# Unread products on TensorE in its waits ahead of the output stage, the expert layers and the second projection

## The chip, the cores and the metric

The kernel runs on one core of one Trainium2 chip. The number that counts is the device time of one execution in microseconds (us). The kernel before takes 3481.51 us (median of 3 runs, 3471.72 to 3489.32).

Engines are named as in the profile: PE is TensorE's stream of matrix products, PEld its loads of the stationary operand, DVE is VectorE, ACT ScalarE, POOL GpSimd, SP the engine that issues most DMAs. Each engine works its instructions in order, and they wait for one another through semaphores.

## The reference, cut to what matters

Two layers over 1024 latent tokens and 256 context tokens, width 1024, all in float32. Each layer is a mixer followed by a mixture of experts:

```python
# layer 0: mixer -> output projection;  layer 1: w_in -> windowed attention -> w_out
x_lat = x_lat + mod_l[2] * o_lat
x_lat = x_lat + mod_l[5] * _ec_moe(_modulate(_rms_norm(x_lat, norm_ffn[i]), mod_l[3], mod_l[4]),
                                   moe_router[i], moe_w1[i], moe_w3[i], moe_w2[i])

def _ec_moe(h, router, w1, w3, w2):     # every expert picks its own best tokens
    aff = softmax(h @ router)           # (tokens, 16 experts)
    gate, idx = top_k(aff.T, 2 * tokens / 16)
    xe = h[idx]
    return scatter_add(idx, (silu(xe @ w1) * (xe @ w3)) @ w2 * gate)
```

So an expert layer can't gather its tokens until the affinities of all tokens are known and sorted: 128 latent tokens for each expert in both layers, and 32 context tokens in layer 0.

## The kernel before, in words

The 1280 tokens are ten tiles of 128 (two of context, eight latent). The stages follow each other in time: a head and the first input projection; the two recurrent mixers and their scan (to 1223 us); the **output stage** of layer 0, which normalizes the mixers' outputs, multiplies by the output weights and computes the router's affinities (to about 1460); the **experts of layer 0** (to 2232); the **second projection**, of layer 1 (to about 2455); attention with its output products (to about 2850); the **experts of layer 1**, and the final norm.

Weights and activations are split into a high and a low half (`split_hl`, L1222 on ACT and L1223 on DVE), and a product is the sum of three products of halves. Those halves have the type float32r. Transposes against the identity matrix `K.ident`, the normalizing products (`post_rwkv`, L1238 and L1243) and the router's products (L1434) use plain float32.

What sets the order around the change: in these stages PE's instructions stand in the order in which the code issues them (`manual_schedule`); the other engines' order is made by a scheduler. The four places are these.

- **Ahead of the output stage.** `block(1)` starts the loads of the scan's results (`s_y`, `s_gb`, `s_o`) for two tiles, and POOL adds the two directions (L1235). Then four generators `post_rwkv` (L1238: a product for the mean; L1243: one for the variance) and two `post_gdn` (L1277: transposes) run, and the output weights `wo` are split. Only then do the output products (L1383) begin.
- **Ahead of the experts of layer 0.** After the last output product the loop over `late` runs what is left of the last two tiles: `ps_af` (L1446, transposes the affinities of a tile), then for the last tile `ps_hT` (L1426, 2 x 4 transposes), `ps_rt` (L1434, 8 router products) and its `ps_af`. DVE sorts in between (`topk_list`, L1459 to L1464). `topk_out` then transposes indices and gates (`ps_tk`, L1521), POOL gathers the tokens by them (L1561, `xe`; L1566, `xce` for context), PE transposes them (`ps_x`, L1580) and the first products of expert 0 begin (`ps_h`, L1611).
- **Ahead of the second projection.** After the last products of the experts (`ps_yc`, L1668) their results are added to `s_x` in memory; then a tile is read back, normalized, transposed (`ps_h`, L1807) and multiplied (`ps_qkv`, L1830; 24 products for a context tile), while the weights `wih`/`wil` are split.
- **Ahead of the experts of layer 1.** The same as in layer 0, without context tokens: `ps_af`, the sort on DVE, `ps_tk`, the gather, `ps_x`, `ps_h`.

Of the kernel before, what the change touches and what calls it, by code (L numbers as in the profile page):

```python
# [9 lines left out]
F32 = mybir.dt.float32  # L10
# [35 lines left out]
def dap(t, off, dims):  # L46
    return bass.AP(tensor=t.tensor, offset=t.offset + off, ap=[list(d) for d in dims])
# [8 lines left out]
def log_exp_table(K):  # L56

    K.table = K.tc.keep_in_program_order(K.nc.scalar.preload_act_table_set("natural_log_exp_and_others")).ins
# [168 lines left out]
def norm_cols(K, pool, layer, norm, ms, mh, tag):  # L227

    nc = K.nc
    G = pool.tile([128, 2, 8, 2], F32, name="G" + tag, bufs=1)  # L230
    for hf in range(2):
        k = slice(4 * hf, 4 * hf + 4)
        nc.vector.scalar_tensor_tensor(
            G[:, 0, k], K.modT[layer][:, ms // 2, :, (ms % 2) * 2 + hf, :], 1.0,
            K.P(norm, 8 * layer + 4 * hf, 4)[:, :, None].to_broadcast([128, 4, 2]), op0=OP.add, op1=OP.mult)
        nc.vector.tensor_copy(G[:, 1, k], K.modT[layer][:, mh // 2, :, (mh % 2) * 2 + hf, :])
    return G
# [982 lines left out]
def split_hl(K, hi, lo, src):  # L1220

    K.nc.scalar.activation(hi, src, AF.Copy)  # L1222
    K.nc.vector.tensor_sub(lo, src, hi)  # L1223
# [59 lines left out]
def turns(posts):  # L1283

    r, g = posts[:4], posts[4:]
    return [r[0], r[1], r[0], r[2], r[1], r[3], r[2], g[0], r[3], g[1]]
# [42 lines left out]
        behind(K, K.nc.sync.dma_start(t[:, k], rows_ap(W, 128 * k * D, 128, D)), last.ins.name)  # L1329


def split_raw(K, wp, raw, name):
    hi = wp.tile([128, 8, D], F32R, name=name + "h")
    lo = wp.tile([128, 8, D], F32R, name=name + "l")
    for k in range(8):
        split_hl(K, hi[:, k], lo[:, k], raw[:, k])
    return hi, lo
# [771 lines left out]
def body(tc, A, out, stop=None, mk=None):  # L2109
    nc = tc.nc  # L2110
    K = Ctx()
    K.nc, K.tc, K.pinned = nc, tc, set()
    with tc.tile_pool(name="consts", reuse_waits="tile", bufs=1) as cp, \
# [85 lines left out]
        with tc.tile_pool(name="moe_io", reuse_waits="tile", bufs=1) as mp:  # L2199
            K.mp = mp  # L2200
            m5 = [None, None]
            with tc.tile_pool(name="post", reuse_waits="tile", bufs=1) as p, \
                    tc.tile_pool(name="ps2", reuse_waits="tile", bufs=2, space=PSUM) as ps2, \
                    tc.tile_pool(name="ps1", reuse_waits="tile", bufs=2, space=PSUM) as ps1:
                log_exp_table(K)
                rt = p.tile([128, 8, 16], F32, name="router")
                nc.sync.dma_start(rt, dap(A["moe_router"], 0, [[16, 128], [2048, 8], [1, 16]]))
                g2 = {}
                nrm = norm_cols(K, mp, 0, "nffn", 4, 3, "f0")
                aff = tp.tile([16, T], F32, name="aff")  # L2210
                tkc = tp.tile([16, 2, 32], F32, name="tkc")
                fill = Fill()
                top = LatTop(K, tp, aff[:, NCTX:], fill, 7)
                late = {}

                def block(b):
                    mh = p.tile([128, 8, 256], F32R, name="mh", tag="mh", bufs=2)
                    ml = p.tile([128, 8, 256], F32R, name="ml", tag="ml", bufs=2)
                    posts = [post_rwkv(K, p, ps1, mh, ml, ct, 256 * b, 256, 0) for ct in range(4)] \
                        + [post_gdn(K, p, ps1, mh, ml, 2 * b + i, 128 * i) for i in range(2)]  # L2220
                    for g in posts:
                        next(g)
                    return mh, ml, turns(posts)

                def rest(o, tt):
                    for _ in range(4):
                        next(o)
                        yield
                    if tt == 1:
                        fill.add(topk_list(K, tp, aff[:, :NCTX], 0, 32, tkc, "c"))  # L2230
                    if tt > 1:
                        top.tile_done(tt)

                with tc.manual_schedule(engines={mybir.EngineType.PE}):
                    nxt = block(1)
                    for g in nxt[2]:
                        next(g)
                    wh, wl = split_raw(K, p, wo, "wo")
                    rawp.close()
                    op = wop.enter_context(tc.tile_pool(name="rows", reuse_waits="tile", bufs=1, side="right"))  # L2240
                    for s in (0, 1):
                        g2[s], = bcast_mods(K, A, 0, s, p, p, ps1, (2,), None, f"o{s}")

                    for at in range(NT):
                        tt = (at + 2) % NT
                        b, i = divmod(tt, 2)
                        if i == 0:
                            mh, ml, _ = nxt
                            q = []
                            if b > 0:  # L2250
                                nxt = block((b + 1) % (NT // 2))
                                q = nxt[2]
                        src = rows_ap(A["ctx"], tt * 128 * D, 128, D) if tt < 2 else \
                            rows_ap(A["x"], (tt - 2) * 128 * D, 128, D)
                        o = slice(128 * i, 128 * i + 128)
                        og = out_tile(K, p, op, ps2, ps1, lambda k, mh=mh, ml=ml, o=o: (mh[:, k, o], ml[:, k, o]), wh, wl, tt, src, g2[int(tt < 2)], nrm, rt, aff, 3, 4)
                        r = rest(og, tt)
                        for k in range(8):
                            next(og)
                            for x in late.pop(8 * at + k, ()):  # L2260
                                next(x, None)
                            if q and k in PSLOT:
                                next(q.pop(0))
                            fill.step(FRATE)
                        for x in RSLOT if at < RCUT else RLAST:
                            late.setdefault(8 * (at + 1) + x, []).append(r)
                        if at == 1:
                            for s in (1, 0):
                                m5[s], = bcast_mods(K, A, 0, s, mp, p, ps1, (5,), None, f"t{s}")
                    for k in sorted(late):  # L2270
                        for x in late[k]:
                            next(x, None)
                lat_sel = top.result(ps1)
                ctx_sel = topk_out(K, tp, ps1, tkc, 32, 4, "c")
            if stop == "out0":
                return
            wop.close()
            with tc.tile_pool(name="moe", reuse_waits="tile", bufs=1) as p, tc.tile_pool(name="mps", reuse_waits="tile", bufs=1, space=PSUM) as ps:
                Moe(K, A, 0, p, ps, lat_sel, ctx_sel, m5, nrm).run()
        if stop == "moe0":  # L2280
            return
        with ExitStack() as kvs:
# [4 lines left out]
            with tc.tile_pool(name="proj", reuse_waits="tile", bufs=1) as p, tc.tile_pool(name="ps2", bufs=3, space=PSUM) as ps2, \  # L2287
                    tc.tile_pool(name="ps1", reuse_waits="tile", bufs=3, space=PSUM) as ps1, \
                    tc.tile_pool(name="psC", reuse_waits="tile", bufs=1, space=PSUM) as psC:
                AT.p = p  # L2290
                afill = Fill()
                pre = stack.enter_context(ExitStack())
                pp = pre.enter_context(tc.tile_pool(name="pre", reuse_waits="tile", bufs=1, side="right"))
                for jj in (1, 2):
                    afill.add(ada_part(K, A, 1, jj, pp, psC))

                def mid():
                    afill.drain()
                    pre.close()
                    AT.kp = kvs.enter_context(tc.tile_pool(name="keys", reuse_waits="tile", bufs=1, side="right"))  # L2300
                    AT.keys(0)
                log_exp_table(K)
                wh, wl = load_split(K, p, A["o_w_in"], D, 1536, "wi", [(k, 0, 128, 128 * k) for k in range(8)], 3, stage=pp)
                mods = norm_cols(K, p, 1, "nmix", 1, 0, "i1")
                with tc.manual_schedule(engines={mybir.EngineType.PE}):
                    AT.project([0, 1] + list(range(2, NT)), wh, wl, mods, ps2, ps1, afill, mid)
                AT.keys(1)
            if stop == "proj":
                return
            with tc.tile_pool(name="tail1", reuse_waits="tile", bufs=1, side="right") as tp, \  # L2310
# [15 lines left out]
                top = LatTop(K, tp, aff, fill, 7, True)  # L2326
# [6 lines left out]
                    top.tile_done(n + 2)  # L2333
                with tc.manual_schedule(engines={mybir.EngineType.PE}):
                    AT.run(ps2, ps1, pso, out_n, fill, split)
                lat_sel = top.result(ps1)
            kvs.close()
            if stop == "out1":
                return
# [34 lines left out]
```

## Time and profile before

| | |
|---|---|
| median of the runs | 3481.51 us |
| lowest and highest | 3471.72 and 3489.32 us |
| the profiled execution: its time | 3488.81 us |
| the profiled execution: its span | 3487.0 us |
| mean granted TensorE clock | 0.945 of full |
| PE busy | 3127.7 us, 90% of the span |
| DVE busy | 2438.2 us, 70% |
| ACT busy | 2074.6 us, 59% |

A row of the timeline is: start in us, duration in us, engine, source line, operation, the tile written <- the tiles read, shape, and how many such records were merged (x8). In brackets stands the idle time of the engine ahead of it and what ended it. A row of the windows is: the stretch, its length, the busy time of each engine in it with the number of its records, the granted TensorE clock as a share of full speed, the share of the DMA engines that was busy, and GB/s. [...] A busy PE isn't a PE at its peak, since a product's duration holds its latency; how long a product occupies PE is read from the starts and ends of its neighbours.

### The profile page before, as it was taken

The page shows a single profiled execution, that of the slowest core. Times are in us where ns is not written, and L with a number is a line of the kernel's source. Part 1 is how long each engine was busy: PE and PEld are TensorE (multiplying, and loading weights), DVE is VectorE, ACT ScalarE, POOL GpSimd, SP SyncE. Part 2 cuts the span into 40 slices and gives each one's busy share as a digit, 9 for nine tenths or more (in the row PEclk, how much of TensorE's full clock was granted, in tenths as well). Part 3 has the DMA queues.
Part 4 walks back from the last instruction along what each step waited for, and adds up shares of the span by engine and source line. Part 5 has one row for each costly group of instructions (what it writes and reads, how often), then busy time and mean ns, then how long its engine had stood idle before and what let it go on. Part 6 is the DMA issues. An engine that isn't in the chain of part 4 may idle for free. (4 is left out here: it accounts for less than half of the span.)

```text
span 3487.0 us, 60267 instructions
## 1 busy us (share of the span) xinstructions
PE 3127.7 (90%) x23392; PEld 2393.5 (69%) x23392; DVE 2438.2 (70%) x4066; ACT 2074.6 (59%) x3548; POOL 726.7 (21%) x716
## 2 busy tenths in 40 slices
PE   5999899995879878699999999799699958999997
PEld 3866667775768757567666767467577746888885
DVE  4268884666534457877777777634876787999998
ACT  4255454332434455477777667534688838888886
POOL 1133332222333343201111110011233310010101
PEclk9999999897889989799999999899899979999998
DMA  5256656666999765578888887662311058999995
GB/s 194 75 181 197 191 194 201 204 187 123 202 221 199 169 218 169 187 254 298 299 286 282 307 287 283 221 212 95 83 49 49 34 205 303 395 384 392 386 380 208
DMA packets 480161, 767.80 MB, mean 220 GB/s; under 512 B 231836, under 2 KB 318532, under 8 KB 472708
## 3 DMA queue, kind: packets, MB, share of 16 engines
q1 hardware_dynamic: 434640, 601.05, 51.5%
q0 software_dynamic: 41648, 151.55, 13.9%
q10 hardware_dynamic: 3587, 11.36, 1.1%
q8 instruction: 184, 3.01, 0.4%
q14 instruction: 102, 0.83, 0.1%
HBM read 631.48 MB, written 132.38 MB: 219 GB/s over the span
## 5 line engine op out<-in xcount | busy, mean ns | idle before, releaser
L1223 DVE TENSOR_TENSOR ulo<-raw,uhi 128x1024 fp32r<-128x1024 f32 x768 | 898.0, 1219 | 84.1 <-ACT uhi L1222 69.7
L1222 ACT ACTIVATE uhi<-raw 128x1024 fp32r<-128x1024 f32 x768 | 790.6, 1073 | 196.6 <-PE ps_y L1662 89.2
L1611 PE MATMUL ps_h<-uhi,xh 128*128 128x512 f32 x1024 | 329.0, 399 | 2.1 <-ACT uhi L1222 2.0
L1611 PE MATMUL ps_h<-ulo,xh 128*128 128x512 f32 x1024 | 319.3, 392 | 3.7 <-DVE ulo L1223 3.0
L1611 PE MATMUL ps_h<-uhi,xl 128*128 128x512 f32 x1024 | 318.6, 392 | 0.0
L1678 POOL DMA_INDIRECT s_x<-yo,idxl x31 | 49.2, 1588 | 945.0 <-DVE yo L1674 945.0
L1611 PEld LDWEIGHTS ps_h<-ulo,xh 128*128 128x128 f32 x1024 | 190.4, 188 | 53.9 <-DVE ulo L1223 12.7
L1611 PEld LDWEIGHTS ps_h<-uhi,xh 128*128 128x128 f32 x1024 | 186.2, 188 | 51.0 <-ACT uhi L1222 8.7
L1611 PEld LDWEIGHTS ps_h<-uhi,xl 128*128 128x128 f32 x1024 | 191.2, 188 | 40.6
L354 PE MATMUL ps_in<-hl,whi 128*128 128x512 f32 x512 | 173.0, 411 | 0.0
L354 PE MATMUL ps_in<-hh,whi 128*128 128x512 f32 x512 | 172.4, 413 | 0.0
L354 PE MATMUL ps_in<-hh,wlo 128*128 128x512 f32 x512 | 171.9, 410 | 0.0
L1662 PE MATMUL ps_y<-uhi,th 128*128 128x512 f32 x512 | 162.1, 397 | 0.7 <-ACT tc L1648 0.6
L1662 PE MATMUL ps_y<-ulo,th 128*128 128x512 f32 x512 | 159.9, 393 | 0.1
L1662 PE MATMUL ps_y<-uhi,tl 128*128 128x512 f32 x512 | 158.1, 390 | 0.0
L1584 ACT ACTIVATE xv<-ps_x,Gf 128x128 f32<-128x128 f32 x256 | 96.9, 471 | 67.0 <-PE ps_x L1580 67.0
L1962 POOL TENSOR_SCALAR pe<-pe,ast 128x640 f32<-128x640 f32 (+1 forms) x48 | 90.2, 1879 | 185.9 <-DVE ast L1961 88.0
L1976 PE MATMUL ps_pT<-ident,pe 128*128 128x128 f32 x608 | 95.9, 282 | 35.1 <-ACT pT L1980 17.2
L852 DVE TENSOR_TENSOR invt<-invB,invX 128x112 f32<-128x112 f32 (+27 forms) x248 | 102.0, 411 | 29.9 <-DMA invB<-s_L 24.6
L1662 PEld LDWEIGHTS ps_y<-uhi,th 128*128 128x128 f32 x512 | 93.7, 188 | 38.9 <-ACT uhi L1222 12.0
L1949 DVE CUSTOM_DVE_ANT_0 pe<-ps_s,amask,sink 128x640 f32<-128x640 f32 (+2 forms) x128 | 103.4, 809 | 24.2 <-PE ps_s L1942 22.8
L1617 PE MATMUL ps_hc<-raw,xc 128*32 128x512 f32 x1024 | 119.6, 596 | 0.0
(505 smaller groups left out, 7276.7 us busy)
## 6 DMA issues: line engine op xcount, KB each, us to landing
raw<-in_moe_w_dram SPq DMA_DIRECT2D x384, 1024.0 KB
ada_w<-in_ada_w_dram SPq DMA_DIRECT2D x48, 1024.0 KB
wraw<-in_e_w_in_dram SPq DMA_DIRECT2D x32, 512.0 KB
s_rk<-arbk POOLq DMA_DIRECT2D x16, 1024.0 KB, 5.2
kq<-s_kq SPq DMA_DIRECT2D x20, 512.0 KB
s_x<-ox POOLq DMA_DIRECT2D x18, 512.0 KB, 3.0
s_h<-ot POOLq DMA_DIRECT2D x18, 512.0 KB, 3.9
s_rkv<-rkv POOLq DMA_DIRECT2D x12, 640.0 KB, 3.9
```

What stands on the lines that cost most here:

```text
L354: nc.tensor.matmul(ps, l[:, k, :], r[:, k, a:a + m], start=(k == 0 and n == 0), stop=(k == 7 and n == 2))
L852: nc.vector.tensor_mul(t, B[:N, k, k + 1:, None].to_broadcast([N, r, c]), X[:N, k, None, 0:c].to_broadcast([N, r, c]))
L1222: K.nc.scalar.activation(hi, src, AF.Copy)
L1223: K.nc.vector.tensor_sub(lo, src, hi)
L1584: nc.scalar.activation(v[:, q], pt[:, q], AF.Identity, bias=self.nrm[:, 1, k, 0:1], scale=self.nrm[:, 0, k, 0:1])
L1611: nc.tensor.matmul(pl[m][n], l[:, k], r[:, 512 * n:512 * n + 512], start=(k == 0 and i == 0), stop=(k == 7 and i == 2))
L1617: nc.tensor.matmul(pc[32 * g:32 * g + 32], xc[:, k_], rs[g // 2][:, 512 * (g % 2):512 * (g % 2) + 512], start=(k_ == 0), stop=(k_ == 7), s ...
L1662: nc.tensor.matmul(py[n], l[:, k], r[:, 512 * n:512 * n + 512], start=(k == 0 and i == 0), stop=(k == 7 and i == 2))
L1678: nc.gpsimd.indirect_dma_start(out=K.s_x[1], out_offset=bass.IndirectOffsetOnAxis(ap=idx[:, e:e + 1], axis=0), in_=yo, in_offset=None, com ...
L1949: nc.vector.tensor_tensor_reduce(pe[:, a:b], sc[:, 512 - nl + a:512 - nl + b], self.mask[:, m:m + b - a], 1.0, low, OP.add, OP.min, st[:, ...
L1962: (nc.vector if n < NV else nc.gpsimd).tensor_scalar(pes[0][:, :nk], pes[0][:, :nk], st[:, 4, 0:1], None, op0=OP.mult)
L1976: nc.tensor.transpose(pt[:, k, i_], pes[i_][:, 128 * (c + k):128 * (c + k) + 128], K.ident)
```

## The change

A new helper issues `n` products of the 128 x 128 identity matrix with itself, in plain float32, into one PSUM tile that nothing reads. It is called at the four places: 36 products ahead of the first normalizing products of the output stage; 16 ahead of every late step and 24 more at the end of that loop; 120 ahead of the second projection; 225 between the last `ps_af` of attention and `ps_tk`, and 40 between `ps_tk` and `ps_x`. In all 557.

```diff
+def warm(K, ps, n, tag="aux"):
+
+    t = ps.tile([128, 128], F32, name="ps_warm", tag=tag)
+    for _ in range(n):
+        K.nc.tensor.matmul(t, K.ident, K.ident, start=True, stop=True)
...
                 with tc.manual_schedule(engines={mybir.EngineType.PE}):
                     nxt = block(1)
+                    warm(K, ps1, 36, "post")
                     for g in nxt[2]:
                         next(g)
...
                     for k in sorted(late):
                         for x in late[k]:
+                            warm(K, ps1, 16, "post")
                             next(x, None)
+                    warm(K, ps1, 24, "post")
                 lat_sel = top.result(ps1)
...
                 with tc.manual_schedule(engines={mybir.EngineType.PE}):
+                    warm(K, ps1, 120)
                     AT.project([0, 1] + list(range(2, NT)), wh, wl, mods, ps2, ps1, afill, mid)
...
                     AT.run(ps2, ps1, pso, out_n, fill, split)
-                lat_sel = top.result(ps1)
+                    warm(K, ps1, 225)
+                    lat_sel = top.result(ps1)
+                    warm(K, ps1, 40)
```

On PE the instructions stand as follows ahead of the experts of layer 0, from the last output products to the first transposed tokens; before:

```order
L1383 MATMUL ps_out<-woh,ml 128x512 x2
L1446 MATMUL ps_af<-ident,sm 16x128
L1426 MATMUL ps_hT<-ident,ot 128x128 x8
L1434 MATMUL ps_rt<-router,ohT 128x16 x8
L1446 MATMUL ps_af<-ident,sm 16x128
L1521 MATMUL ps_tk<-ident,tk_12561 128x16 x2
L1521 MATMUL ps_tk<-ident,tkr 128x16 x2
L1580 MATMUL ps_x<-ident,xe 128x128 x8
```

and with the change, on the same engine at the same place (line numbers are 7 higher behind the new helper; `ps_warm` is its tile):

```order
L1390 MATMUL ps_out<-woh,ml 128x512 x2
L1336 MATMUL ps_warm<-ident 128x128 x16
L1453 MATMUL ps_af<-ident,sm 16x128
L1336 MATMUL ps_warm<-ident 128x128 x32
L1433 MATMUL ps_hT<-ident,ot 128x128 x4
L1336 MATMUL ps_warm<-ident 128x128 x16
L1433 MATMUL ps_hT<-ident,ot 128x128 x4
L1336 MATMUL ps_warm<-ident 128x128 x16
L1441 MATMUL ps_rt<-router,ohT 128x16 x8
L1336 MATMUL ps_warm<-ident 128x128 x16
L1453 MATMUL ps_af<-ident,sm 16x128
L1336 MATMUL ps_warm<-ident 128x128 x40
```

Six runs of the new products, 136 in all, now stand ahead of `ps_tk`, between instructions that depend on one another through DVE and ACT. Ahead of the experts of layer 1, on PE, before:

```order
L1446 MATMUL ps_af<-ident,sm 16x128
L1521 MATMUL ps_tk<-ident,tk_22859 128x16 x2
L1580 MATMUL ps_x<-ident,xe 128x128 x16
L1611 MATMUL ps_h_26931<-uhi,xh 128x512
L1611 MATMUL ps_h_26932<-uhi,xh 128x512
```

and with the change, on the same engine at the same place:

```order
L1453 MATMUL ps_af<-ident,sm 16x128
L1336 MATMUL ps_warm<-ident 128x128 x225
L1528 MATMUL ps_tk<-ident,tk_23161 128x16 x2
L1336 MATMUL ps_warm<-ident 128x128 x40
L1587 MATMUL ps_x<-ident,xe 128x128 x16
```

Nothing but the new products moved on PE here. POOL's order is unchanged; on DVE, ACT and SP a few instructions near the four places change places with a neighbour (in the second projection ACT takes four of the eight `wih` ahead of the first tile's work).

## Rows read from the trace of the kernel before

**Rows 1.** The head of the page.

```profile
span 3487.0 us, 60267 instructions
```

**Rows 2.** Windows, one ahead of each of the four places.

```profile
1230.00:1250.00 20.00, 10.67 (x25) 5.69 (x25) 14.86 (x26) 11.68 (x39) 9.77 (x9) 0.50 0.76 247
1440.00:1470.00 30.00, 12.63 (x53) 9.64 (x53) 20.40 (x74) 11.30 (x31) 6.17 (x7) 0.50 0.75 274
2245.00:2258.00 13.00, 6.94 (x19) 5.09 (x20) 7.32 (x6) 11.90 (x20) 0.00 (x0) 0.50 0.95 361
2840.00:2886.00 46.00, 8.79 (x38) 7.51 (x39) 30.87 (x99) 4.73 (x14) 2.73 (x4) 0.50 0.67 258
```

**Rows 3.** Timeline of PE, in the output stage and at the end of attention.

```profile
1258.98 0.63 PE L1383 MATMUL ps_out<-woh,ml 128*128 128x512 f32 x2
1259.45 0.59 PE L1238 MATMUL ps_mean<-py,hmean 128*128 128x256 f32 x2
1259.69 0.81 PE L1383 MATMUL ps_out<-woh,mh 128*128 128x512 f32 x2
...
2823.95 1.03 PE L1426 MATMUL ps_hT<-ident,ot 128*128 128x128 f32 x8
...
2826.20 1.91 PE L1434 MATMUL ps_rt<-router,ohT 128*128 128x16 f32 x16
```

**Rows 4.** Timeline of PE, ahead of the output stage.

```profile
1222.15 1.04 PE L1168 MATMUL ps_o<-Y,at 64*64 64x128 f32 x16
1230.73 1.22 PE L1238 MATMUL ps_mean<-py,hmean 128*128 128x256 f32 x2 [7.54 <-POOL py L1235]
```

**Rows 5.** Timeline of PE, ahead of the experts of layer 0.

```profile
1434.23 0.28 PE L1446 MATMUL ps_af<-ident,sm 128*16 128x128 f32 x1 [0.81 <-DVE sm L1443]
1440.90 1.97 PE L1426 MATMUL ps_hT<-ident,ot 128*128 128x128 f32 x8 [6.40 <-DVE ot L1418]
1443.62 3.59 PE L1434 MATMUL ps_rt<-router,ohT 128*128 128x16 f32 x16 [0.74 <-ACT ohT L1429]
...
1455.48 0.36 PE L1521 MATMUL ps_tk<-ident,tk 16*128 16x16 f32 x2 [4.33 <-DVE tk L1480]
...
1460.84 1.94 PE L1580 MATMUL ps_x<-ident,xe 128*128 128x128 f32 x8 [0.76 <-DMA xe<-s_h,idxl]
...
1467.06 1.09 PE L1580 MATMUL ps_x<-ident,xe 128*128 128x128 f32 x4 [2.30 <-DMA xe<-s_h,idxl]
1467.80 1.20 PE L1611 MATMUL ps_h<-uhi,xh 128*128 128x512 f32 x2
```

**Rows 6.** Timeline of DVE and PE, ahead of the second projection.

```profile
2231.97 1.96 DVE L1686 SCALAR_TENSOR_TENSOR yc<-ps_yc,gatec,bc5t 32x256 f32<-32x256 f32 x4 [0.71 <-PE ps_yc L1668]
...
2248.08 1.97 PE L1807 MATMUL ps_h<-ident,x 128*128 128x128 f32 x8 [16.18 <-DVE x L1799]
2253.03 0.79 PE L1830 MATMUL ps_qkv<-wih,h1h 128*128 128x512 f32 x1 [2.98 <-ACT h1h L1222]
...
2262.50 0.50 PE L1830 MATMUL ps_qkv<-wil,h1h 128*128 128x512 f32 x1 [1.32 <-DVE wil L1223]
...
2263.07 1.04 PE L1807 MATMUL ps_h<-ident,x 128*128 128x128 f32 x8
```

**Rows 7.** Timeline of PE, ahead of the experts of layer 1.

```profile
2849.21 0.38 PE L1446 MATMUL ps_af<-ident,sm 128*16 128x128 f32 x1 [1.13 <-DVE sm L1443]
2877.45 0.36 PE L1521 MATMUL ps_tk<-ident,tk 16*128 16x16 f32 x2 [27.86 <-DVE tk L1480]
2883.38 3.81 PE L1580 MATMUL ps_x<-ident,xe 128*128 128x128 f32 x16 [5.57 <-DMA xe<-s_h,idxl]
```

**Rows 8.** Windows: experts of layer 0, second projection, experts of layer 1.

```profile
1475.00:2210.00 735.00, 735.00 (x4588) 510.72 (x4587) 551.81 (x566) 519.83 (x737) 77.45 (x54) 1.00 0.80 288
2280.00:2450.00 170.00, 165.18 (x820) 121.23 (x816) 69.47 (x195) 61.84 (x137) 18.72 (x35) 1.00 0.43 146
2890.00:3440.00 550.00, 545.15 (x2480) 441.70 (x2480) 508.14 (x497) 465.62 (x590) 39.87 (x26) 1.00 0.98 369
```

## The prediction

> **What bounds the kernel now.** I read the page's head first: the profiled execution spans 3487.0 us [rows 1] and took 3488.81, which is 7.3 us above the median of the runs, so a sum made in the profile is carried to 3481.51. Then the windows of the stages behind the changed places: the experts of layer 0 keep PE busy 735.00 of 735 us; the second projection 165.18 of 170; the experts of layer 1 545.15 of 550, with the DMA engines at 0.98 [rows 8]. All three run at their own bound from start to end, so a stage that starts later ends later by as much. Ahead of each stands a stretch in which PE waits. [...] Last come the timelines: they show how long each wait is, what ends it, and who waits for the next instruction [rows 4 to 7].
>
> **What one added product costs.** The trace has no plain float32 product of 128 x 128 on the whole array, so I bound it by three neighbours at the full clock.
>
> - The mean's product has twice the columns. The pair of output products ahead of it ends at 1258.98 + 0.63 = 1259.61, the pair behind it at 1259.69 + 0.81 = 1260.50. Of these 0.89 us one pair takes 0.47 (the spacing 1258.98 to 1259.45), so 0.42 are left for 256 columns, and half, 0.21, for 128 [rows 3].
> - Eight router products stream 16 columns each and still take 1.91 us, as sixteen records: 0.24 each with the latency of the last in it, though hardly anything is streamed [rows 3]. An eighth of the columns doesn't make a product cheaper than about 0.2.
> - A transpose of 128 columns is one record, and eight take 1.03 us [rows 3], at most 0.13 each. The mean's product and the router's are two records each; an added product, of their kind, should be two as well: up to 0.26.
>
> I take 0.215 us, next to the halved mean; ends 0.13 (one record) and 0.26. At half clock eight transposes take 1.97 [rows 6] instead of 1.03, so there a product costs about 0.43. All 557 are then 120 us of PE at the full clock. Nobody reads them, but PE works in order, so whatever exceeds a wait delays the next real instruction.
>
> [...]
>
> **Ahead of the output stage: 0 us.** PE is done with the scan at 1222.15 + 1.04 = 1223.2, and the first mean could start when POOL had added the directions, at 1230.73 [rows 4]. 36 x 0.215 = 7.7 us, so until 1230.9: they fill the 7.54 us almost exactly. Behind them PE's sparse work until 1250 (10.67 us busy at half clock) could shrink, if the clock stays up, but DVE is busy 14.86 of those 20 us [rows 2] and most of these PE steps wait for it or ACT. Bounds: 3 us gained to 1 lost.
>
> **Ahead of the experts of layer 0: +6 us.** The last output product ends at 1434.23 - 0.81 = 1433.4 [rows 5]. From there, at the full clock, since PE now never rests: 16 products to 1436.9; `ps_af`; 32 products (6.9) to 1444.0, where the first transposes `ps_hT` stand, which could start at 1440.90; half of them 0.45, 16 products to 1447.9, the other half, 16 products to 1451.8; the router 1.7, to 1453.5 (before: 1443.62 + 3.59 = 1447.2); 16 products to 1457.0; `ps_af`; 40 products (8.6) to 1465.8. `ps_tk` started at 1455.48: +10.3. DVE's sort, which ended that wait, is done long before. The wait for the context's indices shrinks behind it: its `ps_tk`, 4.2 us behind the first one before, follows at once, so that the second gather, on which `ps_x` at 1467.06 and behind it the first expert product at 1467.80 wait, is late by some 6.5 us only. Against it, `ps_x` and the first products, at half clock before, save 1 to 2 us; ACT, which starts on expert 0 a full 10 us late, may take that back. I take +6, bounds +4 to +10.
>
> **Ahead of the second projection: +5 us.** The added products need the PSUM that the experts' last results leave; DVE reads these until 2231.97 + 1.96 = 2233.9. 120 x 0.215 = 25.8, so `ps_h` moves from 2248.08 to 2259.7, +11.7, the wait of 16.18 us notwithstanding [rows 6]. Some comes back. `ps_h` takes 1.0 instead of 1.97. ACT needs 3 us from there to the first `ps_qkv`, a little less where the weights are split already: 2262.2 to 2263.7. The 24 products of the tile took from 2253.03 to 2263.07, at half clock at first and at the end waiting for `wil` (1.32 us at 2262.50) [rows 6]; now all weights are there and they take 24 x 0.235 (half the 0.47 of a pair) = 5.6 us, to 2267.8 to 2269.3. That is 4.8 to 6.2 us behind 2263.07; I take 5. Bounds +1 (attention's first tile hides some) to +12 (nothing comes back).
>
> **Ahead of the experts of layer 1: +24.5 us.** `ps_af` ends at 2849.21 + 0.38 = 2849.6; `ps_tk` waited for the sort until 2877.45, idle 27.86 us [rows 7]. 225 x 0.215 = 48.4 us, plus 2 us because the clock stands at 0.50 when they begin, and may stay there a while, as it did in the projection from 2253.03 to 2258 [rows 2, 6]; 4 us at half clock lose 2: `ps_tk` at 2900, +22.5. The gather, 5.57 us before [rows 7], is now covered by 40 x 0.215 = 8.6, +3. `ps_x` then runs at the full clock and saves about 1. The weights' stream doesn't hide this: the stage is at the DMA's bound [rows 8], and what can be loaded ahead is limited by the 13 `raw` buffers (RAW1), as before. Bounds: +19 to +28.
>
> **Sum.** 0 + 6 + 5 + 24.5 = 35.5 us: in the profile 3488.8 becomes 3524.3, from the median 3481.5 becomes 3517, 1.0% more. The bounds add up to +21 and +51, not all at one end; this case's own range is 3503 to 3532.
>
> **Rivals.**
>
> *The products fit* (not slower). If an added product left one record, like a transpose, it would cost 0.11 to 0.13: 36 take 4.3 us of 7.54; 120 take 14 of 16.18; 225 take 27 of 27.86; 40 take 4.8 of 5.57 [rows 4, 6, 7]. It decides at 0.124 us, where 225 fill the sort's wait. For it speaks that transposes against the same identity have this price; against it, that the mean's and the router's products, of the new ones' kind, have two records each. Then only the clock counts. Halving the 39.0 us [rows 2] gives 19.5 at most; but the steps inside the waits end when DVE, a gather or `wil` lets them, and what is on the path is the first work behind each wait: about 1 us ahead of the output stage, 2 at layer 0, 1 or 2 at the projection, 1 at layer 1. -5 us: 3476.
>
> [...]
>
> *The clock doesn't hold.* If products of an identity matrix left the clock at 0.50, each would cost 0.43: 225 would take 97 us, +69, the 40 +12, the 120 52 and +37, the 136 +44, the 36 +8: about +170, 3650. Against it: plain float32 products ran at the full clock's price between others [rows 3], and the new ones follow each other without a gap.
>
> **How the numbers follow.** The forecast has a chance of 0.83, the fitting products 0.13, the low clock 0.04. Two runs of this kernel can be told apart from 0.5%, 17.4 us, on. Slower by more: 0.84 (nearly all of the first, all of the last). Within: 0.14. Faster by more: 0.02, since even 19.5 us of gain would need every half-speed us on the path. The range 3475 to 3535 takes in the forecast's own range and the upper half of the fitting case.
>
> **What would show it.** In the changed profile `ps_warm` has two records for a product, 1114 in all, at some 0.107 us spacing, and PE shows no wait ahead of `ps_tk` and `ps_x` in layer 1 and of `ps_h` in the projection, but is busy through to them; `ps_tk` of layer 1 starts some 50 us behind `ps_af` instead of 28; the granted clock is 1.00 in the stretches behind. The prediction is wrong if DVE's sort still ends the wait of `ps_tk` in layer 1, or if the experts of layer 1 end as early as before though they start later.

## The result, and the profile after

The changed kernel takes 3521.82 us (median of 4 runs, 3516.32 to 3523.71) beside 3478.19 us for the kernel before (median of 4, 3471.72 to 3489.32). The ratio is 1.0115, 95% interval [1.0099, 1.0132]: 34 to 46 us slower. The profiled execution took 3523.71 us. The head of its page, which answers to [rows 1]:

```profile
span 3521.9 us, 62490 instructions
PE 3237.0 (92%) x24506; PEld 2514.8 (71%) x24506; DVE 2436.3 (69%) x4066; ACT 2074.1 (59%) x3548; POOL 726.0 (21%) x716
```

PE is busy 109 us more than before (3127.7), DVE and ACT within 2 us as long. The view by tile, of the added products (records, shortest, median and longest record in ns, first and last start):

```profile
L1336 PE MATMUL ps_warm<-ident x1114: 272/275/422, 1222.0 to 2922.8; 128*128 128x128 f32 x186
```

1114 records for 557 products: two each. The timeline of PE at the four places, which answers to [rows 4 to 7]; the first fence is ahead of the output stage and of the experts of layer 0:

```profile
1222.03 8.30 PE L1336 MATMUL ps_warm<-ident 128*128 128x128 f32 x72
1230.17 0.60 PE L1238 MATMUL ps_mean<-py,hmean 128*128 128x256 f32 x2
...
1442.63 0.60 PE L1433 MATMUL ps_hT<-ident,ot 128*128 128x128 f32 x4
...
1450.65 1.86 PE L1441 MATMUL ps_rt<-router,ohT 128*128 128x16 f32 x16
...
1456.12 9.10 PE L1336 MATMUL ps_warm<-ident 128*128 128x128 f32 x80
1465.15 0.29 PE L1528 MATMUL ps_tk<-ident,tk 16*128 16x16 f32 x2
1465.29 0.27 PE L1528 MATMUL ps_tk<-ident,tkr 16*128 16x16 f32 x2
1470.57 1.97 PE L1587 MATMUL ps_x<-ident,xe 128*128 128x128 f32 x8 [5.01 <-DMA xe<-s_h,idxl]
...
1474.74 1.22 PE L1618 MATMUL ps_h<-uhi,xh 128*128 128x512 f32 x2 [0.17 <-ACT xh L1222]
```

The waits of `ps_hT` for DVE and of `ps_tk` for the sort (6.40 and 4.33 us in [rows 5]) are gone: PE comes to these instructions later than their inputs do. One wait is left, for the gather, and behind it `ps_x` takes 1.97 us for eight, as long as the eight transposes of [rows 6] at a granted clock of 0.50 [rows 2]. The same view ahead of the second projection and of the experts of layer 1:

```profile
2241.82 27.07 PE L1336 MATMUL ps_warm<-ident 128*128 128x128 f32 x240 [2.08 <-DVE yc L1693]
2268.72 1.04 PE L1814 MATMUL ps_h<-ident,x 128*128 128x128 f32 x8
2272.11 0.50 PE L1837 MATMUL ps_qkv<-wih,h1h 128*128 128x512 f32 x1 [2.35 <-ACT h1h L1222]
...
2278.08 1.04 PE L1814 MATMUL ps_h<-ident,x 128*128 128x128 f32 x8
...
2861.88 0.38 PE L1453 MATMUL ps_af<-ident,sm 128*16 128x128 f32 x1 [1.13 <-DVE sm L1450]
2862.05 51.65 PE L1336 MATMUL ps_warm<-ident 128*128 128x128 f32 x450
2913.63 0.30 PE L1528 MATMUL ps_tk<-ident,tk 16*128 16x16 f32 x2
2913.86 9.20 PE L1336 MATMUL ps_warm<-ident 128*128 128x128 f32 x80
2922.89 1.47 PE L1587 MATMUL ps_x<-ident,xe 128*128 128x128 f32 x12
```

120 products take 2268.72 - 2241.82 = 26.90 us, 0.224 each, at a granted clock of 1.00 (2242.00 to 2268.70). The sort's wait of 27.86 us [rows 7] has become 51.75 us from `ps_af` to `ps_tk`, all of it added products, with no bracket. The windows (stretch, length, busy time of PE, PEld, DVE, ACT and POOL, granted clock, DMA share, GB/s), which answer to [rows 2]:

```profile
1432.00:1465.00 33.00, 33.00 (x298) 32.96 (x296) 25.17 (x86) 5.02 (x14) 3.46 (x3) 1.00 0.67 256
1465.50:1470.50 5.00, 0.07 (x2) 0.00 (x0) 0.39 (x4) 0.00 (x0) 3.66 (x4) 0.81 0.55 143
1470.50:1480.00 9.50, 9.26 (x36) 5.24 (x39) 2.79 (x4) 8.28 (x21) 1.86 (x3) 0.56 0.42 135
2268.70:2278.00 9.30, 6.95 (x34) 5.31 (x33) 3.81 (x4) 6.42 (x15) 0.00 (x0) 1.00 0.76 295
2862.00:2913.00 51.00, 51.00 (x447) 51.00 (x447) 27.00 (x86) 2.11 (x2) 0.00 (x0) 0.97 0.47 186
2923.00:2930.00 7.00, 5.47 (x32) 4.33 (x31) 3.00 (x3) 5.94 (x12) 1.87 (x2) 1.00 0.45 130
```

The clock is up at the projection and at layer 1, at 1.00 behind the added products of both. At layer 0 it was at 1.00 for 33 us; in the gather's wait, 5 us in which PE did two records, it fell again, to 0.81 on average, and it was 0.56 behind it.

**Where the time went.** The work up to the end of the scan is the same in every kernel here, and it ends between 1209.28 and 1225.09 us in the profiles. So the traces are laid on each other at the end of the scan (the end of the last `ps_o` ahead of the output stage: 1223.19 us before, 1222.09 after), and each anchor's shift is counted from there:

| anchor on PE | before, us | after, us | shift | added by the stretch |
|---|---|---|---|---|
| end of the scan | 1223.19 | 1222.09 | 0 | |
| last `ps_out` of layer 0 ends | 1433.41 | 1431.97 | -0.3 | -0.3 |
| last `ps_yc` ends | 2231.90 | 2239.74 | +8.9 | +9.3 |
| first product of attention | 2455.45 | 2468.62 | +14.3 | +5.3 |
| last `ps_af` of attention | 2849.21 | 2861.88 | +13.8 | -0.5 |
| first `ps_h`, experts of layer 1 | 2887.71 | 2926.55 | +39.9 | +26.2 |
| last product of the final norm ends | 3474.26 | 3509.19 | +36.0 | -3.9 |

### The profile page after: what moved, and what is told of

Same layout as the page of the kernel before. It is cut to its first block, busy times and chain, and to the rows that moved or that the text cites. A ratio compares the mean times of both kernels' runs of the same rounds, so it can differ in the third digit from the quotient of the medians.

```text
span 3521.9 us, 62490 instructions
## 1 busy us (share of the span) xinstructions
PE 3237.0 (92%) x24506; PEld 2514.8 (71%) x24506; DVE 2436.3 (69%) x4066; ACT 2074.1 (59%) x3548; POOL 726.0 (21%) x716
## 3 DMA queue, kind: packets, MB, share of 16 engines
q0 software_dynamic: 41648, 151.55, 13.8%
## 5 line engine op out<-in xcount | busy, mean ns | idle before, releaser
L1618 PEld LDWEIGHTS ps_h<-ulo,xh 128*128 128x128 f32 x1024 | 190.8, 188 | 52.3 <-DVE ulo L1223 10.8
L1336 PE MATMUL ps_warm<-ident 128*128 128x128 f32 x1114 | 127.5, 277 | 2.1 <-DVE yc L1693 2.1
L1336 PEld LDWEIGHTS ps_warm<-ident 128*128 128x128 f32 x1114 | 126.6, 194 | 2.9 <-DVE yc L1693 2.6
L1956 DVE CUSTOM_DVE_ANT_0 pe<-ps_s,amask,sink 128x640 f32<-128x640 f32 (+2 forms) x128 | 103.4, 810 | 24.5 <-PE ps_s L1949 23.3
```

The source lines that it names most:

```text
L1336: K.nc.tensor.matmul(t, K.ident, K.ident, start=True, stop=True)
L1618: nc.tensor.matmul(pl[m][n], l[:, k], r[:, 512 * n:512 * n + 512], start=(k == 0 and i == 0), stop=(k == 7 and i == 2))
L1956: nc.vector.tensor_tensor_reduce(pe[:, a:b], sc[:, 512 - nl + a:512 - nl + b], self.mask[:, m:m + b - a], 1.0, low, OP.add, OP.min, st[:, ...
```

## The experiments

The theory is the forecast's: an added product costs about 0.22 us at the full clock, in two records, and what exceeds a wait is paid at each place, while the clock is worth little. Its rivals: something else that came with the products, as another order on the other engines, costs the time; or the clock's value is large and hidden under the overrun.

**One place at a time.** Four kernels keep the added products of one place each. The first:

```diff
                     nxt = block(1)
                     warm(K, ps1, 36, "post")
...
-                            warm(K, ps1, 16, "post")
...
-                    warm(K, ps1, 24, "post")
...
-                    warm(K, ps1, 120)
...
-                    warm(K, ps1, 225)
...
-                    warm(K, ps1, 40)
```

> Only the 36 products ahead of the output stage. Theory overrun (unread products cost 0.224 us each, PE works them in order, and what exceeds a wait delays what stands behind): 36 x 0.224 = 8.1 us against a wait of 7.5 us, so the first mean at most 0.6 us late, the first output product 0 to 1.5 us earlier than before, the end of the kernel within 2 us of before, the time the same. Rival reordering (not the products but the few instructions that change places on DVE, ACT and SP cost the time): some 8 to 15 us slower here too.

The output stage alone: 3475.32 us, ratio 0.9994 [0.998, 1.0008].

> Only the 136 products ahead of the experts of layer 0. Theory overrun: ps_tk 10 to 11 us later than before, the first expert product 7 to 9 us, and the whole kernel 9 us slower, since PE is busy throughout the stage behind. The clock should still be 0.50 at the first expert products, because PE rests over the gather behind ps_tk. Rival reordering: no relation to the 11 us by which ps_tk is late; about a quarter of the whole effect, or nothing.

The 136 ahead of the experts of layer 0: 3492.13 us, 1.004 [1.0022, 1.0059].

> Only the 120 products ahead of the second projection. Theory overrun: 120 x 0.224 = 26.9 us from the moment DVE has read the experts' last results, so the first transposes 12.8 us later than before, the second tile's 7 us (its weights are there, and the first products run at the full clock), the whole kernel about 5 us slower. Rival reordering: the first transposes late, but the end of the kernel not, or by an amount that has nothing to do with it.

The 120 ahead of the projection: 3487.13 us, 1.0016 [0.9999, 1.0033].

> Only the 225 and 40 products around ps_tk ahead of the experts of layer 1. Theory overrun: ps_tk 51.6 us behind ps_af instead of 28 (23.5 us late), ps_x 26.5 us late, and the whole kernel 22 to 26 us slower. Rival reordering: slower by less than 10 us. A second rival, that the weights' stream hides part of it: DMA reads on during the added wait, so that the stage behind is shorter than before by more than 8 us.

The 225 and 40 ahead of the experts of layer 1: 3498.75 us, 1.0067 [1.0046, 1.0087]. The four effects, -0.06, +0.40, +0.16 and +0.67%, add up to 1.17%, beside 1.15% for all at once: within these intervals the places act independently. Counted from the end of the scan, the profiles end later by -1.9, +11.5, +6.8 and +21.4 us, together 37.8, where the changed kernel's ends 36.0 later.

**More of them.** 100 more products where the overrun is largest.

```diff
-                    warm(K, ps1, 225)
+                    warm(K, ps1, 325)
```

> As with 225 and 40 products ahead of the experts of layer 1 alone, with 325 in place of 225; ACT's order is that of the kernel with 225. Theory (a fixed price for each product, all of it on the path): 100 x 0.224 = 22.4 us more between ps_af and ps_tk, and the end of the experts later by 22 to 23 us, the first expert still 59.1. Rival (the longer wait fills the weights' buffers and gives part back): the first expert below 58, the end later by under 20 us.

3534.21 us in the one run. The timeline of PE:

```profile
2850.02 0.38 PE L1453 MATMUL ps_af<-ident,sm 128*16 128x128 f32 x1 [1.14 <-DVE sm L1450]
2850.20 74.49 PE L1336 MATMUL ps_warm<-ident 128*128 128x128 f32 x650
2924.62 0.30 PE L1528 MATMUL ps_tk<-ident,tk 16*128 16x16 f32 x2
```

From `ps_af` to `ps_tk` 74.60 us, beside 52.47 with 225 in the kernel that has this place alone, and 51.75 in the changed one: 22.1 to 22.9 us for 100. From `ps_af` to the end it is 21.9 us more than with 225. Every product behind the sort's end is paid in full, and a still longer wait gives no more back.

**Products that fit.** 280 products, so many at each place as the waits before hold at the measured price.

```diff
...
-                    warm(K, ps1, 36, "post")
+                    warm(K, ps1, 32, "post")
...
+                    room = iter((0, 0, 26, 0, 0, 12, 0))
...
-                            warm(K, ps1, 16, "post")
+                            warm(K, ps1, next(room), "post")
...
-                    warm(K, ps1, 24, "post")
+                    warm(K, ps1, 16, "post")
...
-                    warm(K, ps1, 120)
+                    warm(K, ps1, 60)
...
-                    warm(K, ps1, 225)
+                    warm(K, ps1, 112)
...
-                    warm(K, ps1, 40)
+                    warm(K, ps1, 22)
```

> The same places, but counts that fit the waits at 0.224 us a product: 32 ahead of the output stage; 26, 12 and 16 instead of 136 ahead of the experts of layer 0; 60 instead of 120; 112 and 22 instead of 225 and 40. 280 products in all. Theory overrun: nothing real starts later than before, the overrun of 35 us is gone, and what is left is what the clock is worth: 0 to 8 us faster than before. Rival reordering: still 30 us or more slower, since the same places are touched. Rival, that the products disturb the other engines: DVE's sort or the gathers take longer than before.

3485.28 us, 1.0017 [1.0002, 1.0033]: the overrun of 35 us is gone, but the gain of 0 to 8 us that was expected didn't come; by the interval this kernel is about 1 to 11 us slower than before. The timeline of PE ahead of the experts of layer 1:

```profile
2837.82 27.66 PE L1336 MATMUL ps_warm<-ident 128*128 128x128 f32 x224
2865.80 0.29 PE L1528 MATMUL ps_tk<-ident,tk 16*128 16x16 f32 x2 [0.33 <-DVE tk L1487]
...
2871.39 0.87 PE L1587 MATMUL ps_x<-ident,xe 128*128 128x128 f32 x6 [0.18 <-DMA xe<-s_h,idxl]
```

The sort and the gather end the waits again, 0.33 and 0.18 us behind the last product. In this one profile the work from the end of the scan on is 4.6 us shorter than before, but the runs spread from 3469 to 3491 us, and their interval holds no such gain. The first 1223 us alone differ by as much as 16 us between the profiles; whether the longer runs lose their time there isn't recorded.

**Transposes in their place.** All 557, each with the identity as data, one record each.

```diff
-        K.nc.tensor.matmul(t, K.ident, K.ident, start=True, stop=True)
+        K.nc.tensor.transpose(t, K.ident, K.ident)
```

> All 557, but each as a transpose of the identity (one record) instead of a plain float32 product (two records). Theory overrun: 0.112 us each, 62 us in all instead of 125, so the calls fit into the waits again and the time is within 10 us of before: 225 take 25 us of the 27.9, 40 take 4.5 of 5.6, 120 take 13.4 of the 14 that are left of the third wait; 136 take 15 us, some of it on the path (2 to 4 us). Rival reordering: as slow as with the products, 35 us. Open: whether transposes keep the granted clock at 1.00; if they do the first work behind each wait is at the full clock.

3475.73 us, 0.9989 [0.9975, 1.0003]. The timeline of PE at the same place:

```profile
2841.37 27.34 PE L1336 MATMUL ps_warm<-ident 128*128 128x128 f32 x225
2869.35 0.29 PE L1528 MATMUL ps_tk<-ident,tk 16*128 16x16 f32 x2 [0.64 <-DVE tk L1487]
...
2875.19 1.09 PE L1587 MATMUL ps_x<-ident,xe 128*128 128x128 f32 x8 [1.03 <-DMA xe<-s_h,idxl]
```

225 records in 27.34 us, 0.12 each. In the 21 us from 2847.00 on, at a granted clock of 1.00, there are 194 of them, 0.108 each (this window stands in the last section); the other 31 take the remaining 6.3 us, 0.20 each. These are as many added instructions at the same four places, at the price of the forecast's first rival, and the loss is gone. From the end of the scan on this profile is 4.8 us shorter than before. What cost the time is the length of the added products; that PE's order was changed, or that instructions were added, is not it.

**What gave 3.9 us back.** Behind its late start, layer 1 caught up by 3.9 us within the first expert: from its first `ps_h` to the end of its last `ps_y` it takes 63.1 us before and 59.2 after. From there to the end of the second expert's `ps_y` it is 35.1 us before and 35.4 after, and for each of the next twelve 35.1 to 35.2 in both. The window 2862 to 2913 above holds ACT work, 2.11 us, where before there was none. The timelines of ACT, of the kernel before and then of the one after:

```profile
2884.54 1.50 ACT L1584 ACTIVATE xv<-ps_x,Gf 128x128 f32<-128x128 f32 x4 [35.85 <-PE ps_x L1580]
...
2886.61 1.04 ACT L1222 ACTIVATE uhi<-raw 128x1024 fp32r<-128x1024 f32 x1
```

```profile
2887.30 1.06 ACT L1222 ACTIVATE uhi<-raw 128x1024 fp32r<-128x1024 f32 x1 [25.95 <-DVE tki L1471]
2890.01 1.06 ACT L1222 ACTIVATE uhi<-raw 128x1024 fp32r<-128x1024 f32 x1 [1.66 <-DVE tk L1487]
2923.53 1.50 ACT L1591 ACTIVATE xv<-ps_x,Gf 128x128 f32<-128x128 f32 x4 [32.46 <-PE ps_x L1587]
```

With 225 products the scheduler put two weight splits of expert 0 ahead of `xv` on ACT; before, and in the two kernels whose products fit, they stand behind it. The theory is this order; the rival is that more weights arrive in a longer wait. The first kernel adds no products and puts the two splits first (the products of expert 0 then take their weights from `pre`):

```diff
...
+    def first(self, g):
+        with self.K.tc.manual_schedule(engines={mybir.EngineType.Activation}):
+            its = [self.tiles(self.A[n], 0) for n in ("moe_w1", "moe_w3")]
+            self.pre = [itertools.chain([next(t)], t) for t in its]
+            return self.operands(g)
...
-        x = self.operands(gs[0])
+        x = self.operands(gs[0]) if self.ctx else self.first(gs[0])
```

> The kernel before without added products, with one thing of the kernel after that came with them: on ACT the first two splits uhi<-raw of layer 1's expert 0 stand ahead of the first xv<-ps_x, so that they run in the wait of ps_tk. In before the first expert takes 63.1 us from its first ps_h to the end of its last ps_y, in the kernels with 225 products 59.1 to 59.2. Theory (order on ACT): 59 to 60 here, with the wait still 28 us, and from the end of the scan to the end of the experts 3 to 4 us less than before; total 3474 beside 3478, ratio 0.999. Rival (the longer wait lets more weights arrive): the first expert still takes 63, ratio 1.000.

3478.57 us, 0.9993 [0.9979, 1.0008]. The second keeps the 225 and 40 and puts the splits last; its `first` is

```diff
+            x = self.operands(g)
+            its = [self.tiles(self.A[n], 0) for n in ("moe_w1", "moe_w3")]
+            self.pre = [itertools.chain([next(t)], t) for t in its]
+            return x
```

> 225 and 40 products ahead of the experts of layer 1 alone, and ACT told to do the xv<-ps_x and xh<-xv of expert 0 ahead of every split uhi<-raw, as in before or later. The wait stays long (51 us). Theory (order on ACT): the first expert takes 63 us or more from its first ps_h to the end of its last ps_y, not 59.1. Rival (weights that arrive in the longer wait): 59.

3505.46 us in the one run. Neither came out as expected when counted from the first `ps_h`. In the first kernel the first expert takes 60.9 us, where 59 to 60 were expected, and from the end of the scan to the end the profile is 0.2 us longer than before, where 3 to 4 less were expected. In the second it takes 59.3, where the theory had 63 and the rival 59. But there the loss had moved ahead of that anchor: the first `ps_h` comes 6.8 us behind the first `ps_x`, in the kernel with these places alone 3.7, and from the end of the scan to the end the profile is 25.2 us longer than before, against 21.4. So the count from the first `ps_x` to the end of expert 1's `ps_y` is the better one, chosen after these results:

| kernel | splits on ACT | products | `ps_x` to the end of expert 1 |
|---|---|---|---|
| before; the first three places, each alone | behind `xv` | none in layer 1 | 102.6 us; 102.5 each |
| all transposes | behind | fit | 101.9 |
| products that fit | behind | fit | 101.9 |
| splits last | behind, both `xv` first | 225 + 40 | 102.9 |
| splits early | ahead | none | 100.6 |
| after; layer 1 alone; 325 | ahead | 225 or 325, + 40 | 98.3; 98.2; 98.3 |

Four profiles agree here within 0.1 us, so differences of 0.7 and 2.0 can be read. The order is part of it: with the wait long and the splits last nothing comes back (102.9), which speaks against the rival, though here the splits stand behind both `xv` and so later than before. But the early splits alone bring 2.0 of the 4.3 us. The timelines of PE show the rest; before, then with the splits early, then with the splits last:

```profile
2887.71 0.73 PE L1611 MATMUL ps_h<-uhi,xh 128*128 128x512 f32 x2 [0.51 <-ACT uhi L1222]
2888.97 0.73 PE L1611 MATMUL ps_h<-ulo,xh 128*128 128x512 f32 x2 [0.53 <-DVE ulo L1223]
...
2890.71 0.73 PE L1611 MATMUL ps_h<-uhi,xh 128*128 128x512 f32 x2 [0.55 <-ACT uhi L1222]
...
2927.69 0.73 PE L1611 MATMUL ps_h<-uhi,xh 128*128 128x512 f32 x2 [0.72 <-ACT uhi L1222]
```

```profile
2885.18 1.22 PE L1613 MATMUL ps_h<-uhi,xh 128*128 128x512 f32 x2
2886.20 1.06 PE L1613 MATMUL ps_h<-ulo,xh 128*128 128x512 f32 x2
2887.05 1.06 PE L1613 MATMUL ps_h<-uhi,xl 128*128 128x512 f32 x2
```

```profile
2902.17 0.66 PE L1588 MATMUL ps_x<-ident,xe 128*128 128x128 f32 x4 [0.72 <-ACT xv L1592]
2906.76 1.20 PE L1620 MATMUL ps_h<-uhi,xh 128*128 128x512 f32 x2 [3.94 <-ACT uhi L1223]
```

Before, expert 0's first products wait for splits. With the splits early they don't wait, but a pair now takes 0.85 us from start to start, 2887.05 - 2886.20, at a granted clock of 0.50 (2885.00 to 2889.00), where one takes 0.46 at 1.00 (2892.23 to 2892.69 in the profile before): five pairs, to 2889.61, lose 2.1 us. With the clock up and the splits last, PE waits 3.94 us for ACT (and its clock falls once more, from 0.99 on average between 2900.00 and 2907.00 to 0.82 between 2907.00 and 2916.00: 1.20 us for the pair behind). The clock by itself, with the splits late, is worth the 0.7 us of the table, most of it in `ps_x`. Here are the windows of `ps_x` and of the 4 us behind the first `ps_h` before, and of the same 4 us in the kernel with the 136 products alone:

```profile
2883.00:2887.60 4.60, 3.67 (x16) 3.04 (x16) 0.69 (x1) 3.03 (x7) 1.07 (x2) 0.59 0.31 95
2887.70:2891.70 4.00, 2.70 (x9) 1.31 (x9) 2.91 (x3) 3.97 (x8) 0.71 (x1) 1.00 0.78 247
```

```profile
2889.70:2893.70 4.00, 3.96 (x8) 2.21 (x9) 2.91 (x3) 3.97 (x8) 0.75 (x1) 0.50 0.77 244
```

The clock stands at 1.00 in one and at 0.50 in the other, ACT is busy throughout in both, and the first expert takes 63.1 and 63.0 us. So two covers lie over one stretch, the low clock and the late splits, and taking off one shows the other.

**Both covers off.** Transposes at all places and the splits early, the two edits above together.

> All 557 added products as transposes of the identity, which fit into the waits, and on ACT the first two splits uhi<-raw of layer 1's expert 0 ahead of the first xv<-ps_x. From the first ps_x of layer 1 to the end of expert 1's ps_y, before takes 102.6 us, the kernel after 98.3, the early splits alone 100.6, 225 products with the splits last 102.9. Theory (two covers of one stretch: at half clock the first products of expert 0 are late by themselves, at the full clock ACT's splits are; 2.0 us come back with the splits early, 2.3 more with the clock up as well): 98 to 99 here, with ps_tk still started by DVE's sort about 28 us behind ps_af. From the end of the scan to the end of the experts 6 to 9 us less than before; total 3470 beside 3478, ratio 0.9975, at the edge of what can be measured. Rival (the 4.3 us need the long wait, in which more weights arrive): 100.6 or more, ratio 0.999.

3473.46 us, 0.998 [0.9966, 0.9994]: 2 to 12 us faster than before, and the one kernel here whose interval lies below 1. It overlaps that of the transposes alone, [0.9975, 1.0003], so what the early splits add to them is shown by the profiles only. The timeline of PE:

```profile
2836.15 27.26 PE L1337 MATMUL ps_warm<-ident 128*128 128x128 f32 x225
2864.14 0.29 PE L1529 MATMUL ps_tk<-ident,tk 16*128 16x16 f32 x2 [0.74 <-DVE tk L1488]
...
2874.16 1.22 PE L1620 MATMUL ps_h<-uhi,xh 128*128 128x512 f32 x2
2875.18 0.76 PE L1620 MATMUL ps_h<-ulo,xh 128*128 128x512 f32 x2
2875.78 0.61 PE L1620 MATMUL ps_h<-uhi,xl 128*128 128x512 f32 x2
```

From the first `ps_x` to the end of expert 1: 98.6 us, as expected (98 to 99), with a wait no longer than before; from the end of the scan to the end 7.2 us less (6 to 9 expected). Of the pairs of `ps_h` only the first is that slow here (1.02 us from its start to the next, then 0.60, then 0.45), not five; the granted clock is 0.82 on average from 2874.00 to 2878.00 and 1.00 from there to 2885.00. So the order and the clock together give 4.0 of the 4.3 us back without the long wait, the order alone 2.0 and the clock alone 0.7; the rival, in which the long wait was needed, had 100.6 or more, and falls.

## Why the prediction was right, point by point

The sum was 35.5 us; the profile shows 36.0 from the end of the scan, and the runs 34 to 46. Its terms:

- **The price** was taken as 0.215 us and is 0.224, by two records, inside the bounds of 0.13 and 0.26; over 557 products that is 5 us more of PE. The halved mean was the right neighbour. What sets the price isn't shown: the number of records alone doesn't, since the mean's product costs 0.42 with two records, and the columns alone don't, since the router's, with 16 of them, costs as much as the added one (eight in 1.86 us).
- **The output stage**, 0 predicted: -0.3 to the last output product; alone, 0.9994. Behind 36 products the mean starts 8.08 us after the end of the scan (1230.17 - 1222.09), where it started after 7.54 before: they do fill the wait. The clock behind them was 0.76 on average (1230.00:1249.00), not 1.00.
- **The experts of layer 0**, +6 predicted: +9.3, inside +4 to +10; alone it comes to +11.5 by the end, outside them. `ps_tk` moved by 10.8 us (10.3 predicted) and the context's `ps_tk` by 6.7 (6.5 as the second gather's delay). What failed is the step "`ps_x` and the first products, at half clock before, save 1 to 2 us": no product stands between `ps_tk` and `ps_x` in this layer, the gather left PE idle for 5.01 us, and the clock fell again, to 0.56 on average behind it; the first `ps_h` came 8.0 us late. I had counted on a clock that holds through a wait that the change leaves empty.
- **The second projection**, +5 predicted: +5.3 up to attention. On the way `ps_h` moved by 12.8 us (11.7 predicted) and the second tile by 7.2 (5 predicted); the projection's later tiles gave 2 us of it back.
- **The experts of layer 1**, +24.5 predicted: +26.2 to the first `ps_h`. `ps_af` to `ps_tk` grew by 23.5 us (22.5 predicted): the price added 2 us, and the half clock at its start, taken as 2, cost about 1.5, by the 0.97 over 51 us. The 40 products behind it added 3.3 (3 predicted).
- **"A stage that starts later ends later by as much"** failed in layer 1, by 3.9 us. The step rested on [rows 8], a window of 550 us at the DMA's bound (a share of 0.98). But `ps_x` at half clock (0.59) and the first waits of expert 0 for splits stand ahead of 2890.00, where that window begins, and its later waits (0.55 us ahead of 2890.71, 0.72 ahead of 2927.69) are inside it: a busy time of 545.15 of 550 hides losses of this size. With the splits moved ahead and the clock up, both came back. The forecast looked at PE's order alone ahead of layer 1, and took the two instructions on ACT that changed places for nothing.

So the sum was closer than its terms: 3.3, 0.3 and 1.7 us too low at three places, 3.9 too high at the end. The mechanism, overruns paid in full, is what the runs show; that the total came within 0.5 us, with these errors cancelling, is luck.

The rival of products that fit did not occur with these products, but its price was right for the instruction that it was read from: as transposes the 557 cost 0.12 us each at most, no first work behind a wait came more than 1 us later, and the time came to 0.9989 [0.9975, 1.0003], where it had -5 us, 0.9986. The clock that does not hold was refuted by 0.97 to 1.00 under the products themselves. The 39.0 us that PE is busy in the windows of [rows 2], at a granted clock of 0.50, were worth little here, -0.11% and +0.17% in the two kernels without overrun, whose profiles are 4.8 and 4.6 us shorter behind the scan. Their full worth isn't measured, since neither kernel has the clock up at all four places: in both the first eight `ps_x` of layer 0 take 1.97 us and the first pair of `ps_h` 1.20, where [rows 5] have 1.94 and 1.20 at a granted clock of 0.50 [rows 2]. That the kernel with products that fit is not also faster stays open.

## What to carry to other kernels

Price a filler by the records that it leaves and by a neighbour of its own kind and type (here 0.215 us were taken and 0.224 measured), multiply, and compare the product with each wait in the trace: PE, in order, paid here for every product behind the end of the wait, 22.1 to 22.9 us for 100. Time spent at a low clock is not a gain by itself: beside the 39.0 us before, the two kernels without overrun stand at -0.11% and +0.17%. See whether the first work behind the wait is on the path, and then look for what lies beside it: here the clock and ACT's late splits covered each other, and 0.7 and 2.0 us alone became 4.0 together. Where a scheduler orders the other engines, compare their order at the same places too, since two moved instructions were worth 2 us, and with the clock nearly as much as a term of the sum.

## What was unexpected of the hardware

- The clock fell within a wait of 5.01 us directly behind 33 us of dense products at 1.00: 0.81 on average in the wait, 0.56 in the 9.5 us behind it.
- While PE did nothing but transposes the clock rose, and it stayed up to their end. The window of the 27 us with 225 of them, in the last kernel, granted 0.90, where the same stretch before stood at 0.50 [rows 2]; in the kernel with transposes alone the last 21 us of it were at 1.00:

```profile
2836.00:2863.00 27.00, 27.00 (x224) 27.00 (x225) 26.02 (x83) 1.34 (x2) 0.00 (x0) 0.90 0.89 350
```

```profile
2847.00:2868.00 21.00, 21.00 (x194) 21.00 (x193) 20.55 (x66) 0.00 (x0) 0.00 (x0) 1.00 0.88 349
```

- At the clock 1.00 a float32 product of 128 columns costs 0.224 us (120 in 26.90), and a transpose of the same tile 0.11 (194 records in the 21.00 us above): twice for the same columns, with two records to one.
